# Up projection of the convolutional feed-forward as seven half-size products, gated channels through DRAM, and a down stage that accumulates all channel tiles in eight banks

## The chip, the cores and the metric

The kernel runs on one core of one Trainium2 chip. A core has TensorE (PE, matmuls; PEld is its weight load), VectorE (DVE), ScalarE (ACT), GpSimd (POOL) and SyncE (SP), which here issues the DMAs. SBUF is the working memory, PSUM has eight banks of 128 partitions by 512 float32 into which matmuls accumulate, and DRAM lies outside. The metric is the device time of one execution in microseconds; less is better.

## The reference

One layer of an encoder trunk on 1024 positions with 1024 features: norm, a combined input projection, local and dilated attention, a convolution module and attention to memory tokens, an output projection, and a feed-forward with a convolution. All is float32. The change touches the feed-forward:

```python
f = rms_norm(h, ffn_norm_g[l]) @ w_up[l]          # 1024 x 1024 times 1024 x 5632
f = depthwise_conv(f, ffn_dw_w[l], ffn_dw_b[l])   # 3 taps over positions, one bias a channel
fg, fu = jnp.split(f, 2, axis=-1)                 # 2816 gate channels, 2816 up channels
h = h + (jax.nn.silu(fg) * fu) @ w_down[l]        # 2816 x 1024
```

## The kernel before

Every float32 product is made of three matmuls: each operand is cut into a high part (rounded by ACT to the type `float32r`) and a low part (the operand less its high part, on DVE or POOL), and high x high, high x low and low x high are added in PSUM (`passes`, L140).

Phases 1 and 2 (norm, input projection, attention, convolution, output projection) end with the residual rows in eight SBUF tiles `x_sb` of 128 positions by 1024 features. The last rounds of the output projection add into them from PSUM (`add_out`, L1071). They are not changed.

Phase 3 begins at L1098. Constants are loaded and transposed (L1103 to L1113). For each of the eight tiles of positions, ACT squares and sums the row (L1120), POOL makes the inverse root (L1121 calls `rsqrt`, L163 and L164), DVE scales into a new tile `xn` (L1122), PE transposes it in two halves (L1127), ACT writes the high part of the transpose (L1129) and DVE the low part (L1130). The two tiles `hT` hold this for all positions: [feature, position tile, feature tile, 128 positions].

`up(ct)` (L1137) makes one tile of 128 channels by 1024 positions. Its weights come in two loads of 256 KB (`up_raw`, L1142, two buffers), each cut into a high part by ACT (L1146) and a low part by POOL (L1147). Then 8 feature tiles x 3 parts x 2 halves of the positions make 48 matmuls into two banks (L1152). Three taps of the convolution follow, read from the banks: ACT makes the middle tap with the bias (L1159), DVE the others (L1160 to L1165). There are 44 such tiles of channels: tile ct of the first 22 is a gate, tile 22 + ct what it gates.

`gated(ct)` (L1169) calls `up` for both, ACT applies SiLU (L1171), DVE multiplies (L1173), ACT and DVE cut the product into parts (L1175, L1176), which stay in SBUF.

`down(gs, cts, last)` (L1189) takes two gated tiles at a time: for each position tile and each half of the output features, six matmuls go into one of two banks (L1195), and DVE adds the bank to `x_sb` (L1198): 16 banks for each two tiles, 176 in all. The weights come by L1184 and are cut by L1185 and L1186. The last call sends `x_sb` to the output (L1200). The outer loop (L1202 to L1209) traces `gated` for two tiles and then `down` for the two before.

What sets the order: the program is traced as above, and a scheduler at compile time (`schedule_with_timeline_sim=True`, L1229) puts each engine's instructions in a fixed order. An instruction traced earlier goes first where both are ready by the scheduler's own clock; one that isn't ready lets a later one pass. On the chip each engine then works through its fixed list, and waits at the first instruction whose inputs or buffers aren't there. SP issues the DMAs of phase 3 in one such list, too. Tiles of one tag share a number of buffers (`bufs`), and a new tile waits until the buffer's old readers are done.

Of the kernel before, what the change touches and what calls it, by code (L numbers as in the profile page):

```python
# [9 lines left out]
F = mybir.dt.float32  # L10
# [15 lines left out]
# tiles of 4 KB that the steps share: how many a step may hold, and how many are kept for it  # L26
# [4 lines left out]
# the order of the input projections, the number of them before the first head  # L31
ORDER = "q0 kv g0 g1 v0 q1 v1 q2 m q3".split()
HEAD0 = 2
# steps after each tap of the two tiles of the conv module
PACE = (1, 2)
# tiles of weights whose low parts DVE makes
EARLY = 12
# steps whose instructions go before others, or after them
PRIOS = {"softmax_weights": 1000, "memory_values": -60, "memory_heads": 60, "add_out": 200}
# tiles of mixed rows in the rounds of the output projection  # L40
# [3 lines left out]
def constants():  # L44
    """What depends on shapes alone. Token n = 128 b + 64 e + 16 r + s of a tile stands for
    position 128 b + 64 e + 4 s + r, so that the tokens of one residue mod 4 are runs of 16."""
    c = {}
# [85 lines left out]
def block(tc, a, out):  # L133
# [6 lines left out]
    def passes(n):  # L140
        """(stationary part, moving part) of a float32 product, parts 0: high, 1: low."""
# [19 lines left out]
    def rsqrt(dst, src, scale):  # L161
        """(src * scale + eps) ** -0.5"""
# [61 lines left out]
    def scores(t, ps, mask, nm, den):  # L224
        """one block of 128 queries and 256 keys -> exp(s - max), with -max and the sum"""
# [1007 lines left out]
```

## Time and profile before

| | |
|---|---|
| median of 3 runs | 1340.15 us (1337.95 to 1342.56) |
| span of the profiled execution | 1341.0 us |
| PE, DVE, ACT, POOL busy in it | 94%, 57%, 39%, 38% |
| mean granted TensorE clock | 0.978 |
| first matmul of the up projection, last one of the down projection | 587.5 us, 1335.9 us |
| matmuls of the up projection (L1152), of the down projection (L1195) | 2112, 1056 |

How to read the lines that follow. A page of the profile gives the span, the busy time of each engine and, in 40 slices, the busy tenths and the granted clock (PEclk). A table by stretches (windows) gives for each stretch its length and, for each engine, busy time and (x) instructions begun in it, then the granted clock, the share of the DMA engines and GB/s. A view of one source line gives count, durations in ns as least/median/most, first and last start, and shapes. The timeline gives start in us, duration in us, engine, line, operation, tiles (out<-in), count, and in brackets the idle time before it with what ended it. The list of waits gives total us, times and the longest. A matmul's recorded duration (0.39 us) is longer than the distance to the next one, since they are pipelined: rates are read from counts over stretches.

### The profile page before, as it was taken

The numbers are of one execution on the slowest core, as the hardware profiler recorded it, in microseconds if no ns is written. First come the engines' busy times: TensorE is split into PE (matmuls) and PEld (weight loads), VectorE is DVE, ScalarE is ACT, GpSimd is POOL, SyncE is SP. The second block draws the span as 40 slices with busy tenths as digits, with TensorE's granted clock in tenths as the row PEclk, the third lists the DMA queues.
The fourth block names the chain that finished last, engine by engine and source line by source line (L and its number), as shares of the span: only waits on it lengthen the run. The fifth ranks groups of instructions, "written<-read, shape, count | busy, mean of one in ns | idle before, by whom it ended". The sixth has DMA issues, their size and how long they took to land.

```text
span 1341.0 us, 18723 instructions
## 1 busy us (share of the span) xinstructions
PE 1260.7 (94%) x6895; PEld 1055.1 (79%) x6895; DVE 768.3 (57%) x1530; ACT 521.5 (39%) x1082; POOL 513.2 (38%) x647
## 2 busy tenths in 40 slices
PE   4999897899899989889999999999999999999998
PEld 4988897899768767668888887878787878787876
DVE  7836888786788769883443434434344343434454
ACT  5664163476757656453421313131313131313120
POOL 5723783897655442431410404040405050505010
PEclk9999988999989999999999999999999999999999
DMA  8263426362773331101310303030303030303013
GB/s 271 82 173 95 147 83 197 119 186 80 240 240 95 95 107 36 50 17 33 101 40 0 95 1 94 0 95 0 95 1 94 2 94 0 95 1 87 8 32 126
DMA packets 130039, 114.27 MB, mean 85 GB/s; under 512 B 6850, under 2 KB 110108, under 8 KB 129948
## 3 DMA queue, kind: packets, MB, share of 16 engines
q1 hardware_dynamic: 129948, 113.08, 27.7%
q8 instruction: 54, 0.88, 0.3%
q14 instruction: 37, 0.30, 0.1%
HBM read 87.89 MB, written 25.17 MB: 84 GB/s over the span
## 4 chain that ended last, share of the span: by engine, by line
issue 31%; PE 27%; DMA 17%; POOL 11%; DVE 7%; ACT 5%; SPq 1%; POOLq 0%; ACTq 0%; DVEq 0%
DMA up_raw<-w_up 8%; PE ps_up L1152 7%; PE proj L883 6%; PE proj L1062 5%; POOL up_lo L1147 3%; DMA dn_raw<-w_down 3%; POOL dn_lo L1186 3%; POOL prob L339 2%; PE o L274 2%; PE turn L265 2%; PE s L245 2%; DMA w_raw<-w_in 2%; ACT up_hi L1146 1%; PE ps_dn L1195 1%; DVE conv L946 1%
## 5 line engine op out<-in xcount | busy, mean ns | idle before, releaser
L1152 PE MATMUL ps_up<-hT,up_hi 128*128 128x512 f32 x1408 | 399.8, 396 | 0.0
L1152 PEld LDWEIGHTS ps_up<-hT,up_hi 128*128 128x128 f32 x1408 | 264.2, 188 | 63.6
L1198 DVE TENSOR_TENSOR x<-ps_dn,x 128x512 f32<-128x512 f32 x176 | 120.5, 688 | 204.9 <-PE ps_dn L1195 204.8
L1152 PE MATMUL ps_up<-hT,up_lo 128*128 128x512 f32 x704 | 228.9, 395 | 0.0
L1186 POOL TENSOR_TENSOR dn_lo<-dn_raw,dn_hi 128x512 fp32r<-128x512 f32 x44 | 65.2, 1490 | 406.4 <-ACT dn_hi L1185 406.4
L883 PE MATMUL proj<-w_hi,hnT 128*128 128x256 f32 x896 | 192.0, 302 | 18.3 <-ACT raw L798 6.5
L1147 POOL TENSOR_TENSOR up_lo<-up_raw,up_hi 128x512 fp32r<-128x512 f32 x88 | 121.0, 1377 | 152.6 <-ACT up_hi L1146 148.3
L1160 DVE SCALAR_TENSOR_TENSOR y<-ps_up,fwT,y 128x511 f32<-128x511 f32 x88 | 65.1, 746 | 186.4 <-ACT y L1159 186.4
L883 PEld LDWEIGHTS proj<-w_hi,hnT 128*128 128x128 f32 x896 | 154.0, 204 | 21.1 <-ACT raw L798 7.1
L1152 PEld LDWEIGHTS ps_up<-hT,up_lo 128*128 128x128 f32 x704 | 132.3, 188 | 31.6
L1159 ACT ACTIVATE y<-ps_up,fwT 128x512 f32<-128x512 f32 x88 | 63.8, 771 | 207.3 <-PE ps_up L1152 206.0
L1195 PE MATMUL ps_dn<-dn_hi,g_hi 128*128 128x512 f32 x352 | 138.5, 394 | 4.6 <-DVE x L1198 4.6
L1195 PE MATMUL ps_dn<-dn_lo,g_hi 128*128 128x512 f32 x352 | 138.0, 392 | 0.3 <-POOL dn_lo L1186 0.3
L1195 PE MATMUL ps_dn<-dn_hi,g_lo 128*128 128x512 f32 x352 | 138.1, 392 | 0.0
L883 PE MATMUL proj<-w_lo,hnT 128*128 128x256 f32 x448 | 134.2, 300 | 0.3 <-POOL w_lo L605 0.3
L1062 PE MATMUL proj<-w_hi,mx 128*128 128x512 f32 x256 | 101.0, 431 | 7.5 <-DVE x L1072 5.7
L1146 ACT ACTIVATE up_hi<-up_raw 128x512 fp32r<-128x512 f32 x88 | 55.7, 632 | 125.4 <-DMA up_raw<-w_up 104.5
L339 POOL TENSOR_SCALAR prob<-prob,wc 128x256 f32<-128x256 f32 x128 | 76.6, 620 | 42.6 <-DVE wc L335 42.6
L883 PEld LDWEIGHTS proj<-w_lo,hnT 128*128 128x128 f32 x448 | 91.1, 203 | 1.2 <-POOL w_lo L605 1.0
L617 POOL TENSOR_TENSOR w_lo<-w_raw,w_hi 128x512 fp32r<-128x512 f32 x44 | 64.1, 1469 | 58.7 <-ACT w_hi L615 55.8
L1195 PEld LDWEIGHTS ps_dn<-dn_hi,g_hi 128*128 128x128 f32 x352 | 66.1, 188 | 24.4 <-DVE x L1198 10.0
L946 DVE SCALAR_TENSOR_TENSOR conv<-conv,cwT 128x1009 f32<-128x1009 f32 (+14 forms) x60 | 83.9, 1399 | 0.6
(201 smaller groups left out, 2084.4 us busy)
## 6 DMA issues: line engine op xcount, KB each, us to landing
up_raw<-w_up SPq DMA_DIRECT2D x88, 256.0 KB
dn_raw<-w_down SPq DMA_DIRECT2D x44, 256.0 KB
x<-x SPq DMA_DIRECT2D x16, 512.0 KB
qk_d<-out SPq DMA_DIRECT2D x32, 256.0 KB
qk<-qk_d SPq DMA_DIRECT2D x16, 512.0 KB
w_raw<-w_in SPq DMA_DIRECT2D x40, 128.0 KB
qk<-qk_d SPq DMA_DIRECT2D x16, 256.0 KB
v_d<-out SPq DMA_DIRECT2D x16, 256.0 KB
```

The source lines that it names most:

```text
L339: pool.tensor_scalar(probs[u], probs[u], wc[:, u : u + 1], 0.0, OP.mult, OP.add)
L617: (dve if next(chunk_no) < EARLY else pool).tensor_tensor(lo, raw, f32(hi), OP.subtract)
L883: pe.matmul(ps[:, :256], lhs[i][:, k], c.parts[k][j], start=(k == 0 and i == 0 and j == 0), stop=(k == KT - 1 and i == 1))
L946: dve.scalar_tensor_tensor(acc[:, c0:c1], conv_in[i][:, c0 + k - 15 : c1 + k - 15], w, acc[:, c0:c1], OP.mult, OP.add)
L1062: pe.matmul(ps, mixed[k][i][:, 128 * t : 128 * t + 128], wo[k, half][j], start=(n == 0), stop=(n == 3 * len(ks) - 1))
L1146: act.activation(hi, raw, AF.Copy)
L1147: pool.tensor_tensor(lo, raw, f32(hi), OP.subtract)
L1152: pe.matmul(pss[half], w[k][i], hT[j][:, 4 * half : 4 * half + 4, k], start=(k == 0 and i == 0 and j == 0), stop=(k == KT - 1 and i == 1))
L1160: dve.scalar_tensor_tensor(y[:, c0 + 1 : c1], ps[:, 0:511], tap3[0], y[:, c0 + 1 : c1], OP.mult, OP.add)
L1186: pool.tensor_tensor(w[1][:, cut], raw, f32(w[0][:, cut]), OP.subtract)
L1195: pe.matmul(ps, gs[k][i][:, 128 * t : 128 * t + 128], ws[k][j][:, 512 * half : 512 * half + 512], start=(n == 0), stop=(n == 3 * len(cts) ...
L1198: dve.tensor_tensor(dst, ps, dst, OP.add)
```

## The change

Phases 1 and 2 stay. Phase 3 is written anew; the diff also strips comments, which is left out here.

The up projection of a pair of column tiles (gate tile ct, up tile 22 + ct) is a product of a 2 x 2 matrix of blocks, A (two halves of the positions by two halves of the features), with a 2 x 2 matrix of blocks B (two halves of the features by the two column tiles). It is made in Winograd's form of Strassen's method with seven half-size products in place of eight. Each product is 4 feature tiles x 3 parts = 12 matmuls of 512 positions. The seven left operands (A11, A12, A22 and the sums S1 to S4) are made once for all pairs, after the norm, which now scales `x_sb` in place; the rows before the norm go to DRAM (`h_d`). The seven right operands are B11, B21, B22 and the differences T1 to T4, made by DVE for each pair; all seven are cut into parts, high by ACT, low by POOL. Raw blocks have five buffers of 256 KB, sums and differences four, high and low parts eight each. Banks a, b and c have two buffers, bank d takes one of two single banks in turn. Three banks are accumulated into twice, with a read between (a: p1, then the first half of the gate; c: p5; d: the second half of the up tile). The convolution now reads whole rows from SBUF (`cg`, `cu`) in place of halves in PSUM. The gated tile is not cut but stored to DRAM (`g_d`).

The down stage begins when all 22 pairs are traced. For each half of the positions, all eight banks hold one output block each, over all 22 channel tiles; gated tiles and weights come from DRAM and are cut on the way, the weights in each half anew. A bank is added to the old rows, loaded from `h_d`, once, and the result stored.

```diff
-        hT = [p3r.tile([128, NT, KT, 128], R, name=f"hT{i}") for i in range(2)]
...
+        ops = {nm: [p3r.tile([128, KH, HT], R, name=f"{nm}{i}") for i in range(2)]
+               for nm in ("A11", "A12", "A22", "S1", "S2", "S3", "S4")}
+        ss2 = p3r.tile([128, NT], F, name="ss2")
+        def turn_rows(rows, nm, t):
+            ps = psp.tile([128, KH, 128], F, name="ps_n", tag="turn", bufs=2)
+            for k in range(KH):
+                pe.transpose(ps[:, k], rows[:, 128 * k : 128 * k + 128], ident)
+            hi, lo = (x[:, :, 128 * t : 128 * t + 128] for x in ops[nm])
+            act.activation(hi, ps, AF.Copy)
+            dve.tensor_tensor(lo, ps, f32(hi), OP.subtract)
+        def norm(t):
+            sp.dma_start(h_d[t], x_sb[t])
+            sq = p3r.tile([128, D], F, name="sq2", tag="wide", bufs=2)
+            col = ss2[:, t : t + 1]
+            act.activation(sq, x_sb[t], AF.Square, accum_out=col)
+            rsqrt(col, col, 1.0 / D)
+            xns[t] = x_sb[t]
+            dve.scalar_tensor_tensor(x_sb[t], x_sb[t], col, g_ffn, OP.mult, OP.mult)
         for t in range(NT):
+            norm(t)
+            if t < 4:
+                turn_rows(xns[t][:, 0:512], "A11", t)
+                turn_rows(xns[t][:, 512:1024], "A12", t)
+        for t in range(4):
+            lowr, high = xns[t], xns[t + 4]
+            s1, s2, s3, s4 = (p3r.tile([128, 512], F, name=f"s{i}", tag="wsum", bufs=4) for i in range(4))
+            dve.tensor_tensor(s3, lowr[:, 0:512], high[:, 0:512], OP.subtract)
+            turn_rows(s3, "S3", t)
+            dve.tensor_tensor(s1, high[:, 0:512], high[:, 512:1024], OP.add)
+            turn_rows(s1, "S1", t)
+            dve.tensor_tensor(s2, s1, lowr[:, 0:512], OP.subtract)
+            turn_rows(s2, "S2", t)
+            dve.tensor_tensor(s4, lowr[:, 512:1024], s2, OP.subtract)
+            turn_rows(s4, "S4", t)
+            turn_rows(high[:, 512:1024], "A22", t)
+        xpool.release()
+        pu = tc.alloc_tile_pool(name="pu", bufs=1)
+        BANKS = {"a": ("s", 2), "b": ("proj", 2), "c": ("turn", 2)}
+        def split(src, shape, adder):
+            hi = wpool.tile(shape, R, name="up_hi", tag="w_hi", bufs=8)
+            lo = wpool.tile(shape, R, name="up_lo", tag="w_lo", bufs=8)
+            act.activation(hi, src, AF.Copy)
+            adder.tensor_tensor(lo, src, f32(hi), OP.subtract)
+            return hi, lo
+        def up_weights(ct):
...
+            b11, b12 = load(0, ct), load(0, NF + ct)
+            w["B11"] = split(b11, shape, pool)
+            t1 = comb(b12, b11)
+            b22 = load(1, NF + ct)
+            t3 = comb(b22, b12)
+            t2 = comb(b22, t1)
+            b21 = load(1, ct)
+            w["B21"] = split(b21, shape, pool)
+            w["T3"] = split(t3, shape, pool)
+            w["T1"] = split(t1, shape, pool)
+            t4 = comb(b21, t2)
+            w["T2"] = split(t2, shape, pool)
+            w["B22"] = split(b22, shape, pool)
+            w["T4"] = split(t4, shape, pool)
+        def product(ps, x, w, first, last):
+            for n, (k, i, j) in enumerate(passes(range(KH))):
+                pe.matmul(ps, w[i][:, k], ops[x][j][:, k], start=(first and n == 0), ...)
         def gated(ct):
-            fg = up(ct)
-            act.activation(fg, fg, AF.Silu)
-            fu = up(NF + ct)
+            w = up_weights(ct)
+            cg, cu = (pu.tile([128, S], F, name=nm, tag="c", bufs=3) for nm in ("cg", "cu"))
+            p1, p5, u2, v = (pu.tile([128, 512], F, name=nm, tag="part", bufs=6) for nm in ("p1", "p5", "u2", "v"))
+            pa = bank("a", ct)
+            product(pa, "A11", w["B11"], True, True)
+            act.activation(p1, pa, AF.Copy)
+            pd = bank("d", ct)
+            product(pd, "S3", w["T3"], True, True)
+            product(pa, "A12", w["B21"], False, True)
+            act.activation(cg[:, 0:512], pa, AF.Copy)
+            pc = bank("c", ct)
+            product(pc, "S1", w["T1"], True, True)
+            act.activation(p5, pc, AF.Copy)
+            pb = bank("b", ct)
+            product(pb, "S2", w["T2"], True, True)
+            dve.tensor_tensor(u2, pb, p1, OP.add)
+            pool.tensor_tensor(v, u2, p5, OP.add)
+            dve.tensor_tensor(cu[:, 512:1024], pd, v, OP.add)
+            product(pc, "S4", w["B22"], False, True)
+            dve.tensor_tensor(cu[:, 0:512], pc, u2, OP.add)
+            product(pd, "A22", w["T4"], False, True)
+            dve.tensor_tensor(cg[:, 512:1024], pd, u2, OP.add)
+            ys = []
+            for c, col in ((cu, NF + ct), (cg, ct)):
+                y = p3r.tile(..., tag="wide", bufs=2) if c is cu else pu.tile([128, S], F, name="yg", bufs=2)
+                act.activation(y, c, AF.Identity, scale=tap[1], bias=b)
+                dve.scalar_tensor_tensor(y[:, 1:S], c[:, 0 : S - 1], tap[0], y[:, 1:S], OP.mult, OP.add)
+                dve.scalar_tensor_tensor(y[:, 0 : S - 1], c[:, 1:S], tap[2], y[:, 0 : S - 1], OP.mult, OP.add)
+            act.activation(fg, fg, AF.Silu)
             dve.tensor_tensor(fg, fg, fu, OP.mult)
-            hi, lo = (p3.tile([128, S], R, name=nm, tag=nm, bufs=4) for nm in ("g_hi", "g_lo"))
-            act.activation(hi, fg, AF.Copy)
-            dve.tensor_tensor(lo, fg, f32(hi), OP.subtract)
-            return hi, lo
+            sp.dma_start(g_d[ct], fg)
+        DBANKS = [("s", 2), ("s", 2), ("proj", 2), ("proj", 2), ("turn", 2), ("turn", 2), ("o", 1), ("z", 1)]
+        for part in range(2):
+            banks = [psp.tile([128, 512], F, name="ps_dn", tag=tag, bufs=n) for tag, n in DBANKS]
+            for k in range(NF):
+                gk = split(half_raw(g_d[k][:, HT * part : HT * part + HT]), [128, 512], dve)
+                wk = [split(half_raw(a["w_down"][0, 128 * k : 128 * k + 128, 512 * half : 512 * half + 512]), [128, 512], pool)
+                      for half in range(2)]
+                for n, ps in enumerate(banks):
+                    t, half = n // 2, n % 2
+                    for m, (i, j) in enumerate(((0, 0), (0, 1), (1, 0))):
+                        pe.matmul(ps, gk[i][:, 128 * t : 128 * t + 128], wk[half][j],
+                                  start=(k == 0 and m == 0), stop=(k == NF - 1 and m == 2))
+            for n, ps in enumerate(banks):
+                t, half = 4 * part + n // 2, n % 2
+                r = pu.tile([128, 512], F, name="res", tag="part", bufs=6)
+                sp.dma_start(r, h_d[t][:, 512 * half : 512 * half + 512])
+                dve.tensor_tensor(r, ps, r, OP.add)
+                sp.dma_start(out[128 * t : 128 * t + 128, 512 * half : 512 * half + 512], r)
```

More of the change, by code (lines that the diff above doesn't have):

```diff
@@ L1096, in block @@
     p2.release()
+    h_d = [dpool.tile([128, D], F, name=f"h_d{t}") for t in range(NT)]
+    g_d = [dpool.tile([128, S], F, name=f"g_d{ct}") for ct in range(NF)]
     with (
         tc.tile_pool(name="p3r", bufs=1, side="right") as p3r,
-        tc.tile_pool(name="p3", bufs=1) as p3,
     ):
-        g_ffn = p3r.tile([128, D], F, name="g_ffn", tag="y", bufs=4)
+        g_ffn = p3r.tile([128, D], F, name="g_ffn", tag="wide", bufs=2)
         sp.dma_start(g_ffn, bass.AP(tensor=a["ffn_norm_g"].tensor, offset=0, ap=[[0, 128], [1, D]]))
-        fw = p3r.tile([2 * NF, 4, 128], F, name="fw", tag="y", bufs=4)
+        fw = p3r.tile([2 * NF, 4, 128], F, name="fw", tag="raw", bufs=5)
         sp.dma_start(fw[:, 0:3], a["ffn_dw_w"][0].rearrange("k (t p) -> t k p", p=128))
@@ L1113, in block @@
         dve.tensor_copy(fwT, ps[:, :, : 2 * NF])
[L1115 removed]
+        HT = S // 2
+        KH = KT // 2
+        ops = {nm: [p3r.tile([128, KH, HT], R, name=f"{nm}{i}") for i in range(2)]
+               for nm in ("A11", "A12", "A22", "S1", "S2", "S3", "S4")}
         ss2 = p3r.tile([128, NT], F, name="ss2")
[L1117 to L1130 removed]
@@ new lines, in product, with bank @@
+        def product(ps, x, w, first, last):
+            for n, (k, i, j) in enumerate(passes(range(KH))):
+                pe.matmul(ps, w[i][:, k], ops[x][j][:, k], start=(first and n == 0), stop=(last and n == 3 * KH - 1),
+                          skip_group_check=not first)
+        def bank(which, ct):
+            if which == "d":
+                return psp.tile([128, 512], F, name="ps_d", tag="oz"[ct % 2], bufs=1)
+            tag, n = BANKS[which]
+            return psp.tile([128, 512], F, name="ps_" + which, tag=tag, bufs=n)
@@ L1171, in gated @@
             act.activation(fg, fg, AF.Silu)
-            fu = up(NF + ct)
             dve.tensor_tensor(fg, fg, fu, OP.mult)
-            hi, lo = (p3.tile([128, S], R, name=nm, tag=nm, bufs=4) for nm in ("g_hi", "g_lo"))
-            act.activation(hi, fg, AF.Copy)
-            dve.tensor_tensor(lo, fg, f32(hi), OP.subtract)
-            return hi, lo
-        def down_weights(ct):
-            w = [p3.tile([128, D], R, name=nm, tag=nm, bufs=3) for nm in ("dn_hi", "dn_lo")]
-            for half in range(2):
-                cut = slice(512 * half, 512 * half + 512)
-                raw = wpool.tile([128, 512], F, name="dn_raw", tag="w_raw", bufs=2)
-                sp.dma_start(raw, a["w_down"][0, 128 * ct : 128 * ct + 128, cut])
-                act.activation(w[0][:, cut], raw, AF.Copy)
-                pool.tensor_tensor(w[1][:, cut], raw, f32(w[0][:, cut]), OP.subtract)
-            return w
@@ L1189, in down @@
-        def down(gs, cts, last):
-            ws = [down_weights(ct) for ct in cts]
-            for t in range(NT):
-                for half in range(2):
-                    ps = psp.tile([128, 512], F, name="ps_dn", tag="proj", bufs=2)
-                    for n, (k, i, j) in enumerate(passes(range(len(cts)))):
-                        pe.matmul(ps, gs[k][i][:, 128 * t : 128 * t + 128], ws[k][j][:, 512 * half : 512 * half + 512],
-                                  start=(n == 0), stop=(n == 3 * len(cts) - 1))
-                    dst = x_sb[t][:, 512 * half : 512 * half + 512]
-                    dve.tensor_tensor(dst, ps, dst, OP.add)
-                if last:
-                    sp.dma_start(out[128 * t : 128 * t + 128, :], x_sb[t])
@@ L1202, in block, with half_raw @@
-        before = None
-        for c in range(NF // 2):
-            cts = [2 * c, 2 * c + 1]
-            gs = [gated(ct) for ct in cts]
-            if before:
-                down(*before, False)
-            before = (gs, cts)
-        down(*before, True)
-    xpool.release()
+            sp.dma_start(g_d[ct], fg)
+        for ct in range(NF):
+            gated(ct)
+        DBANKS = [("s", 2), ("s", 2), ("proj", 2), ("proj", 2), ("turn", 2), ("turn", 2), ("o", 1), ("z", 1)]
+        def half_raw(src):
+            t = p3r.tile([128, 512], F, name="dn_raw", tag="raw", bufs=5)
+            sp.dma_start(t, src)
+            return t
@@ L1211, in block @@
+        pu.release()
     wpool.release()
```

62 lines of the change are left out of this document (16 added, 46 removed).

## The prediction

> **What bounds the kernel now.** I read the page first, then the table by stretches around phase 3, then the counts of its two matmul lines, PE's waits, and last the views of single lines.
>
> ```profile
> span 1341.0 us, 18723 instructions
> PE 1260.7 (94%) x6895; PEld 1055.1 (79%) x6895; DVE 768.3 (57%) x1530; ACT 521.5 (39%) x1082; POOL 513.2 (38%) x647
> ```
> ```profile
> 560.00:570.00 10.00, 5.88 (x16) 3.81 (x15) 8.24 (x9) 3.96 (x6) 3.22 (x2) 0.70 0.37 114
> 570.00:587.00 17.00, 13.64 (x67) 9.34 (x66) 16.32 (x24) 9.61 (x19) 6.57 (x12) 0.98 0.01 1
> ...
> 735.00:1290.00 555.00, 550.35 (x2360) 442.21 (x2359) 226.34 (x360) 140.95 (x199) 143.53 (x100) 1.00 0.16 48
> 1290.00:1336.00 46.00, 45.74 (x198) 36.33 (x196) 26.16 (x39) 3.66 (x5) 2.54 (x2) 1.00 0.19 76
> ```
> ```profile
> 734.40:748.40 14.00, 13.98 (x60) 11.27 (x60) 1.00 0.26 76
> ```
> ```profile
> 1292.00:1312.00 20.00, 20.00 (x88) 15.83 (x87) 1.00 0.00 0
> 1314.00:1334.00 20.00, 19.74 (x86) 15.64 (x85) 1.00 0.40 158
> ```
> ```profile
> PE ps_dn L1195 <- DVE x L1198: 4.6, 7, 1.6
> ```
>
> From 735 to 1290 us PE is busy 550.35 of 555 us at full clock, while DVE is busy 41%, ACT and POOL 26%. The third fence is L1152 alone, in a stretch without down matmuls: 14.00 / 60 = 0.2333 us each. The fourth is L1195 alone: 20.00 / 88 = 0.2273 us. PE's longest wait in phase 3 comes to 4.6 us. So phase 3 is bound by the number of matmuls, and only what shortens or interrupts that stream counts.
>
> **Matmuls removed.** A pair of column tiles takes 96 matmuls now and 7 x 12 = 84 then; over 22 pairs 2112 become 1848. 264 x 0.2333 = **-61.6 us**. The down projection keeps its 1056.
>
> **Their rate.** L1152 streams four runs of 128 positions, L1195 one run of 512; the new products stream one run of 512. If that is the 0.0060 us between the rates, 1848 x 0.0060 = 11.1 us more go; if not, nothing. I take **-5**.
>
> **Down stage.** Each bank is added once, 16 adds for 176: the 4.6 us of waiting end, since each new bank is left alone for the other seven (7 x 3 x 0.2273 = 4.8 us) before it is needed. What is new is the feed: 24 matmuls (5.45 us) use three raw blocks of 256 KB, 144 GB/s, where 158 GB/s took 0.40 of the DMA engines.
>
> ```profile
> 760.15 2.77 DMA dn_raw<-w_down
> ```
> ```profile
> L1184 SPq DMA_DIRECT2D dn_raw<-w_down x44: 327/328/346, 641.1 to 1287.4; - x44
> ```
> ```profile
> L1146 ACT ACTIVATE up_hi<-up_raw x88: 618/632/650, 491.7 to 1232.1; 128x512 fp32r<-128x512 f32 x88
> ```
> ```profile
> L1147 POOL TENSOR_TENSOR up_lo<-up_raw,up_hi x88: 1274/1293/2249, 492.4 to 1232.8; 128x512 fp32r<-128x512 f32 x88
> ```
>
> A raw buffer turns in 0.33 + 2.77 + 0.63 + 1.29 = 5.0 us (6.0 with POOL's slowest), so five supply three blocks in 3.0 to 3.6 us, under 5.45. The feed binds only from a turn of 9.1 us. I take **-4**, ends -5 and +8.
>
> **Head of the stage.** All sums of rows must stand before the S products.
>
> ```profile
> 589.69 0.48 PE L1152 MATMUL ps_up<-hT,up_hi 128*128 128x512 f32 x1
> ...
> 600.92 0.60 PE L1127 MATMUL ps_n<-small,xn 128*128 128x128 f32 x4
> 601.28 0.48 PE L1152 MATMUL ps_up<-hT,up_hi 128*128 128x512 f32 x1
> ```
> ```profile
> 586.75 0.68 DVE L1072 TENSOR_TENSOR x<-proj,x 128x512 f32<-128x512 f32 x1
> 587.34 1.28 DVE L1122 SCALAR_TENSOR_TENSOR xn<-x,ss,g_ffn 128x1024 f32<-128x1024 f32 x1
> 588.54 0.68 DVE L1130 TENSOR_TENSOR hT<-ps_n,hT 128x512 fp32r<-128x512 f32 x1
> 589.14 0.68 DVE L1072 TENSOR_TENSOR x<-proj,x 128x512 f32<-128x512 f32 x1
> ...
> 592.93 0.68 DVE L1130 TENSOR_TENSOR hT<-ps_n,hT 128x512 fp32r<-128x512 f32 x1
> ```
>
> DVE is already full here (16.32 of 17 us), with starts 0.60 us apart, 1.20 for the norm. Up to about 593 us it does what it did. Then one norm, 20 low parts and 16 sums are left, 1.2 + 36 x 0.60 = 22.8 us, so the last operand stands near 616 us, 619 at the operations' own lengths, more with weight differences between. The last position tile takes nine of these steps, so its S3 is ready some 4 us before that, at 612 to 615. Until then PE has only A11 of two pairs (bank a has two buffers): p1, which A12 waits for, lies in the old rows' space, last read near the end too. Before, PE streamed from 589.7 with eight groups of transposes (0.36 us each by the rows) between. I let the stream begin at 615.5, for the weight differences; that loses 25.8 - 24 x 0.2333 - 8 x 0.36 = 17.3; with the store to `h_d`, which the in-place norm must await, I take **+18**. Ends: +10 if some sums are made before 593, +35, twice the estimate, if the space of the old rows or of the new operands comes free late. The first raw blocks may stand behind the eight stores on SP, but B11 is wanted only with A11, near 589.
>
> **The exposed chain in each pair.** A22 accumulates onto bank d, which must first be read: S2's end, u2 (DVE), v (POOL), the second half of cu (DVE), then PE.
>
> ```profile
> L1198 DVE TENSOR_TENSOR x<-ps_dn,x x176: 675/691/694, 683.8 to 1336.4; 128x512 f32<-128x512 f32 x176
> ```
> ```profile
> L1122 DVE SCALAR_TENSOR_TENSOR xn<-x,ss,g_ffn x8: 1275/1276/2073, 572.4 to 598.1; 128x1024 f32<-128x1024 f32 x8
> ```
> ```profile
> L617 DVE TENSOR_TENSOR w_lo<-w_raw,w_hi x12: 676/688/1218, 21.6 to 77.9; 128x512 fp32r<-128x512 f32 x12
> ```
> ```profile
> L1159 ACT ACTIVATE y<-ps_up,fwT x88: 760/771/779, 599.5 to 1291.8; 128x512 f32<-128x512 f32 x88
> ```
> ```profile
> L1171 ACT ACTIVATE y<-y x22: 1042/1059/1065, 628.8 to 1285.9; 128x1024 f32<-128x1024 f32 x22
> ```
> ```profile
> 756.35 1.30 POOL L1147 TENSOR_TENSOR up_lo<-up_raw,up_hi 128x512 fp32r<-128x512 f32 x1 [2.09 <-ACT up_hi L1146]
> 757.88 2.25 POOL L1147 TENSOR_TENSOR up_lo<-up_raw,up_hi 128x512 fp32r<-128x512 f32 x1 [0.22 <-ACT up_hi L1146]
> ```
> ```profile
> 756.36 0.69 DVE L1198 TENSOR_TENSOR x<-ps_dn,x 128x512 f32<-128x512 f32 x1
> 756.96 0.74 DVE L1165 SCALAR_TENSOR_TENSOR y<-ps_up,fwT,y 128x512 f32<-128x512 f32 x1
> 757.74 1.23 DVE L1173 TENSOR_TENSOR y<-y 128x1024 f32<-128x1024 f32 x1
> ```
>
> Alone the chain is 0.69 + 1.29 + 0.69 = 2.7 us and a few hops; S4 covers 12 x 0.2333 = 2.8. But engines may be taken: DVE by a tap (1.28), POOL by a low part (1.29). So it lasts 2.8 to 5.4, and shows 0 to 2.5 us a pair, where PE's list holds no matmul of the next pair in that place. The list does mix work so:
>
> ```profile
> 734.19 0.39 PE L1195 MATMUL ps_dn<-dn_hi,g_lo 128*128 128x512 f32 x1
> 734.42 0.63 PE L1152 MATMUL ps_up<-hT,up_lo 128*128 128x512 f32 x2
> ```
>
> I take 0.8 us, nearer the low end because A11 of the next pair is there to be put in: 22 x 0.8 = **+18**, ends 0 and 55.
>
> The other engines are loaded per pair (PE 84 x 0.2333 = 19.6 us): DVE 4 x 0.69 weight differences + 4 x 0.69 from banks + 4 x 1.28 taps (as long as the norm's L1122, of the same operation) + 1.23 gate = 11.8; POOL 8 x 1.29 = 10.3; ACT 7 x 0.63 + 3 x 0.77 + 3 x 1.06 = 9.9. So these are hidden, as are the reads of banks a (S3 between p1 and A12: 2.8 us) and c (S2 between p5 and S4). Behind v in POOL's list stand low parts of the next pair, with eight buffers for seven operands some five products (14 us) ahead. On SP the store of the gated tile waits for the gate, and the next raw blocks stand behind it with the same lead. Should that cover go, each late block costs its 2.77 us. The traffic, 1.0 MB in and 0.5 MB out in 19.6 us, is 80 GB/s, half of the 158 shown.
>
> The last two fences show the catch: POOL takes 1.30 us beside DVE operations that read PSUM, but 2.25 beside the product of two SBUF tiles. Such operations grow from 1.23 x 2 a pair (this product and g_lo, of the same shape) to 2.75 + 5.1 + 1.23 = 9.1 us; with POOL's 10.3 that is 19.4 of PE's 19.6. The Trainium skill ("SBUF — State Buffer", section "SBUF: two separate sides") has a rule against this change: GpSimd and a VectorE operation with two SBUF inputs share a port pair under an exclusive lock, and the later one blocks. The trace agrees: the 2.25 us are 1.29 and nearly all of the 1.09 us overlapped.
>
> **Seams and tail.** From up to down and between the two halves: **+2** (0 to 6), since all but the last gated tiles lie in DRAM by then.
>
> ```profile
> 1336.35 0.69 DVE L1198 TENSOR_TENSOR x<-ps_dn,x 128x512 f32<-128x512 f32 x1 [0.67 <-PE ps_dn L1195]
> ```
>
> After 1337.04 the last 512 KB took to 1341.0; 256 KB take **-1** (to 0).
>
> **Sum.** -61.6 - 5 - 4 + 18 + 18 + 2 - 1 = -33.6 on 1341.0: 1307.4. The median lies 0.85 below this execution, so 1306.6, said as 1307.
>
> **Rivals.**
> - *The port pair binds* (chance 0.14). For: 19.4 of 19.6 us leaves nothing for an in-order list that idles. Against: weights are made some 14 us ahead, so both lists can shift without PE noticing. With a tenth idle a pair takes 21.4, 1.8 more: 22 x 1.8 = 40 in place of 18 gives 1329.
> - *A22 waits out the chain* (0.12), the slower end. Without the exposed term the sum is -51.6, so it decides from 51.6 / 22 = 2.35 us a pair. If v stands behind a low part stretched to 2.25 us and is stretched itself, and u2 behind a tap: 1.28 + 0.69 + 2.25 + 2.25 + 0.69 - 2.8 = 4.4 at worst; at 3.4 it is 1341 - 52 + 75 = 1364. For: the fixed list cannot know these stretches. Against: PE's waits are now 4.6 us in all under the same scheduler.
> - *Nothing shows* (0.10): contiguous rate, +10 head, 0.2 us a pair: -61.6 - 11.1 - 5 + 10 + 4.4 + 0 - 1 = -64.3, 1277.
> - *The clock falls* (0.03). In 560 to 570 us PE, busy 5.88 of 10, got 0.70:
>
> ```profile
> 563.84 0.71 PE L1062 MATMUL proj<-w_hi,mx 128*128 128x512 f32 x1 [1.19 <-DVE mx L280]
> 566.51 0.80 PE L1062 MATMUL proj<-w_hi,mx 128*128 128x512 f32 x1 [1.96 <-DVE x L1072]
> ```
>
> If breaks hold the up stage (431 us) at 0.9, it costs 48: 1341 - 52 + 18 + 48 = 1355. The Trainium skill ("TensorE: Matmul & The Clock Gate", Part 1) halves the clock after an idle window of about 3.4 us; by that, breaks of one or two microseconds would cost nothing, though the two rows are such breaks in the stretch at 0.70.
> - *The feed binds the down stage* (0.03): a turn of 10 us makes 6.0 of 5.45, 44 x 0.55 = +24, 1331.
>
> **How the numbers follow.** The forecast has 0.58, most of it 1285 to 1330. A measurement here tells 0.3%, 4 us. Faster: 0.56 of it, 0.11 of the port's, 0.10 where nothing shows and 0.03 where the feed binds, 0.80. Within 1336 to 1344: 0.02 of it, 0.03 of the port's, 0.01 of the chain's just past its point, 0.06. Slower: the chain's 0.11 and the clock's 0.03, 0.14. The range, 1279 to 1344, leaves out these 0.14 and half of "nothing shows".
>
> **What would show it.** Right: up matmuls near 0.228 to 0.233 us over full stretches; the stream full from about 615 us; 20 to 21 us a pair; a down stage near 240 us with PE full; POOL lengths bimodal. Wrong: a break over 2.35 us before each A22; POOL or DVE busy over 90% in the up stage; PE waiting for low parts; clock under 1 after 620 us.

## The result, and the profile after

| | before | after |
|---|---|---|
| median of 4 runs | 1340.53 us | 1318.91 us (1316.23 to 1320.34) |
| ratio, 95% interval | | 0.9841 (0.9822 to 0.986) |
| profiled execution, span | 1341.0 us | 1316.23 us, span 1314.5 us |

Faster by 21.6 us; the forecast was 1307, the range 1279 to 1344. The page of after:

```profile
span 1314.5 us, 19197 instructions
PE 1205.7 (92%) x6679; PEld 1007.3 (77%) x6679; DVE 905.2 (69%) x1420; ACT 608.6 (46%) x1248; POOL 760.1 (58%) x779
```

PE lost 55 us of busy time, but 2% of its share too: part of what the removed matmuls gave is idle time now. The table by stretches shows where:

```profile
570.00:587.00 17.00, 5.71 (x23) 3.55 (x21) 12.43 (x12) 11.72 (x22) 11.54 (x17) 0.62 0.51 175
587.00:597.00 10.00, 6.22 (x23) 4.76 (x24) 8.82 (x13) 3.18 (x6) 1.86 (x2) 0.50 0.00 1
...
700.00:1050.00 350.00, 338.56 (x1432) 267.43 (x1431) 277.96 (x221) 149.85 (x222) 234.41 (x138) 1.00 0.26 78
1080.00:1180.00 100.00, 100.00 (x442) 82.79 (x442) 23.89 (x19) 30.34 (x54) 56.61 (x39) 1.00 0.48 155
```

From 570 to 587 us DVE, full in that stretch before, is busy 12.43 of 17, and the granted clock is 0.62, then 0.50. In the up stage (700 to 1050) PE misses 11.4 us of 350. The down stage (last row) has no gap: 442 matmuls in 100.00 us, by their starts one every 0.2267 us.

The four longest in PE's list of waits from 570 us on:

```profile
PE ps_d L1206 <- DVE cu L1233: 11.4, 17, 0.7
PE ps_n L1129 <- DVE A L1132: 9.4, 8, 3.1
PE ps_n L1129 <- DVE S L1132: 8.1, 13, 1.1
PE ps_n L1115 <- DMA fw<-ffn_dw_w: 5.2, 1, 5.2
```

The first is the exposed chain, in 17 of the 22 pairs (from 700 us on); the others are the head.

The two executions had drifted apart by 6.0 us when attention ended (last matmul of L274 at 556.7 and 550.7), before anything that was changed. So the stages are counted from there, by the first and last starts in the views of the matmul lines; "down alone" and the last two columns are experiments, below:

| us after the last matmul of attention | before | after | down alone | two pools | three edits |
|---|---|---|---|---|---|
| last matmul of the output projection | 31.8 | 19.5 | 31.1 | 28.0 | 28.3 |
| last up matmul | 734.2 | 520.9 | 527.6 | 510.6 | 497.0 |
| last down matmul | 779.2 | 755.1 | 767.0 | 744.5 | 730.7 |
| end | 784.3 | 763.8 | 771.1 | 752.6 | 734.9 |

784.3 - 763.8 = 20.5 us, about the 21.6 of the medians. This gain is made up of five terms:

- count of matmuls: -61.6;
- down stage, and breaks of the old alternation of up and down: -11.2 (what the other terms leave; measured alone below);
- head: +32.1 (the stream is full 74.1 us after attention for 33.0; 9.0 us are taken off for 26 matmuls and eight groups of transposes that lie before it; two matmuls lay before it in the old kernel too, which is 0.5 us);
- breaks in the pairs: +16.6;
- tail: +3.6.

### The profile page after: what moved, and what is told of

Read it like the earlier page. It is cut to its first block, busy times and chain, and to the rows that moved or that the text cites. A ratio compares the mean times of both kernels' runs of the same rounds, so it can differ in the third digit from the quotient of the medians.

```text
span 1314.5 us, 19197 instructions
## 1 busy us (share of the span) xinstructions
PE 1205.7 (92%) x6679; PEld 1007.3 (77%) x6679; DVE 905.2 (69%) x1420; ACT 608.6 (46%) x1248; POOL 760.1 (58%) x779
## 4 chain that ended last, share of the span: by engine, by line
PE 55%; DVE 13%; POOL 9%; issue 8%; DMA 7%; ACT 7%; SPq 1%; POOLq 0%; DVEq 0%; ACTq 0%
PE ps_dn L1271 17%; PE proj L1062 6%; PE ps_c L1206 6%; PE ps_d L1206 6%; PE ps_a L1206 5%; PE proj L883 4%; PE ps_b L1206 3%; DMA w_raw<-w_in 2%; PE o L274 2%; DVE up_sum L1183 2%; POOL r L164 2%; PE turn L265 2%; PE proj L909 2%; DVE yg L1248 2%; PE s L245 2%
## 5 line engine op out<-in xcount | busy, mean ns | idle before, releaser
L1171 POOL TENSOR_TENSOR up_lo<-up_sum,up_hi 128x512 fp32r<-128x512 f32 x88 | 164.3, 1877 | 62.0 <-ACT up_hi L1170 58.4
L1171 POOL TENSOR_TENSOR up_lo<-dn_raw,up_hi 128x512 fp32r<-128x512 f32 x88 | 131.2, 1510 | 115.3 <-ACT up_hi L1170 102.1
L1170 ACT ACTIVATE up_hi<-dn_raw 128x512 fp32r<-128x512 f32 x132 | 75.3, 622 | 162.8 <-issue 119.6
L1271 PE MATMUL ps_dn<-up_lo,up_hi 128*128 128x512 f32 x352 | 136.9, 389 | 0.1
L1271 PE MATMUL ps_dn<-up_hi,up_lo 128*128 128x512 f32 x352 | 136.5, 389 | 0.0
L1271 PE MATMUL ps_dn<-up_hi 128*128 128x512 f32 x352 | 133.4, 389 | 0.0
L1206 PE MATMUL ps_a<-A,up_hi 128*128 128x512 f32 x352 | 115.2, 399 | 0.0
L1206 PE MATMUL ps_c<-S,up_hi 128*128 128x512 f32 x352 | 110.9, 396 | 0.7 <-DVE S L1132 0.7
L1206 PEld LDWEIGHTS ps_a<-A,up_hi 128*128 128x128 f32 x352 | 66.7, 190 | 16.1
L1271 PEld LDWEIGHTS ps_dn<-up_lo,up_hi 128*128 128x128 f32 x352 | 66.1, 188 | 14.3 <-POOL up_lo L1171 0.6
```

Of the source, the lines that this page charges most:

```text
L1170: act.activation(hi, src, AF.Copy)
L1171: adder.tensor_tensor(lo, src, f32(hi), OP.subtract)
L1206: pe.matmul(ps, w[i][:, k], ops[x][j][:, k], start=(first and n == 0), stop=(last and n == 3 * KH - 1), skip_group_check=not first)
L1271: pe.matmul(ps, gk[i][:, 128 * t : 128 * t + 128], wk[half][j], start=(k == 0 and m == 0), stop=(k == NF - 1 and m == 2))
```

## The experiments

Ratios are to the kernel before on the same chip; "after" means 0.9841.

**The tail.** After's last two adds wait for their old rows. The last matmul, the last load, and the last add:

```profile
1305.79 0.39 PE L1271 MATMUL ps_dn<-up_hi,up_lo 128*128 128x512 f32 x1
1306.48 0.61 SPq L1276 DMA_DIRECT2D res<-h_d  x1
1310.83 0.69 DVE L1277 TENSOR_TENSOR res<-ps_dn,res 128x512 f32<-128x512 f32 x1 [2.51 <-DMA res<-h_d]
```

A row of `res` can be loaded only when one of six buffers has been stored. Experiment: the last two in another tag.

```diff
-r = pu.tile([128, 512], F, name="res", tag="part", bufs=6)
+r = pu.tile([128, 512], F, name="res", tag="part" if n < 6 else "c", bufs=6 if n < 6 else 3)
```

> The last two of the eight old-row blocks are loaded into buffers of another tag (the freed convolution rows), in place of waiting for the first two results to be stored. If the tail is held by these buffers (in the changed kernel 8.3 us from PE's last matmul to the end, against 4.7 before): the last additions follow PE at once, the tail falls to about 4.5 us, 1315.3 us against 1318.9. If the landing of the last stores sets the end whatever the loads do: at most 1 us less, 1318 to 1319.

Measured: 0.9809 (0.9794 to 0.9824), 0.0032 of 1340 or 4.3 us below after. The timeline's end:

```profile
1298.59 5.45 DVE L1277 TENSOR_TENSOR res<-ps_dn,res 128x512 f32<-128x512 f32 x8 [9.65 <-PE ps_dn L1271]
```

All eight adds run together, and the end comes 4.7 us after the last matmul for 8.7. The buffers were the cause.

**The breaks in the pairs.** One pair in the timeline of after, DVE, POOL and the matmul that waits:

```profile
875.01 1.28 DVE L1243 SCALAR_TENSOR_TENSOR yg<-cg,fwT,yg 128x1023 f32<-128x1023 f32 x1
875.58 4.12 POOL L1171 TENSOR_TENSOR up_lo<-up_sum,up_hi 128x512 fp32r<-128x512 f32 x2 [1.38 <-ACT up_hi L1170]
876.33 2.20 DVE L1244 SCALAR_TENSOR_TENSOR yg<-cg,fwT,yg 128x1023 f32<-128x1023 f32 x1
878.45 1.79 DVE L1183 TENSOR_TENSOR up_sum<-up_raw 128x512 f32<-128x512 f32 x1
880.16 0.68 DVE L1183 TENSOR_TENSOR up_sum<-up_raw,up_sum 128x512 f32<-128x512 f32 x1
880.28 1.72 POOL L1171 TENSOR_TENSOR up_lo<-up_raw,up_hi 128x512 fp32r<-128x512 f32 x1 [0.59 <-ACT up_hi L1170]
880.76 2.31 DVE L1248 TENSOR_TENSOR yg<-yg,yu 128x1024 f32<-128x1024 f32 x1
883.00 0.68 DVE L1231 TENSOR_TENSOR u<-ps_b,p 128x512 f32<-128x512 f32 x1
883.82 1.30 POOL L1232 TENSOR_TENSOR v<-u,p 128x512 f32<-128x512 f32 x1 [1.82 <-DVE u L1231]
885.16 0.69 DVE L1233 TENSOR_TENSOR cu<-ps_d,v 128x512 f32<-128x512 f32 x1 [1.48 <-POOL v L1232]
885.90 0.73 PE L1206 MATMUL ps_d<-A,up_hi 128*128 128x512 f32 x2 [0.66 <-DVE cu L1233]
```

S2's last matmul ends at 876.6. The chain itself (883.00 to 885.9) takes 2.9 us, as the forecast had it; but u2 starts 6.4 us late, behind a tap, two differences and the gate product. Those that ran beside POOL's low parts took 2.20, 1.79 and 2.31 us; without POOL they take 1.28, 0.69 and 1.23. PE had 37 matmuls (8.6 us) of other products to put between, not quite enough. Two readings: DVE's list is simply too long there, or the port pair stretches it. Two experiments take POOL's low parts away: onto DVE, which makes DVE's list longer, or onto ACT, as a copy in the low part's place (this leaves out the subtraction of the high part).

```diff
-            adder.tensor_tensor(lo, src, f32(hi), OP.subtract)
+            (dve if shape[1] == KH else adder).tensor_tensor(lo, src, f32(hi), OP.subtract)
```

> All seven low parts of a pair's weights are made by DVE, none by POOL; POOL keeps v. Port theory (u2 comes late because DVE's taps, differences and gate product ahead of it are stretched while POOL reads SBUF): DVE has 16.6 us of 19.6 a pair but no stretch, taps 1.28 and not 2.2 us, the break ahead of A22 falls from 0.94 to about 0.3 us a pair, 10 to 15 us less, 1304 to 1309. List theory (u2 is late because of what stands ahead of it in DVE's list, stretched or not): more stands ahead of it now, the break grows by one or two low parts, 0.7 to 1.4 us a pair, 15 to 30 us more, 1334 to 1349.

```diff
-            adder.tensor_tensor(lo, src, f32(hi), OP.subtract)
+            if shape[1] == KH:
+                act.activation(lo, src, AF.Copy)
+            else:
+                adder.tensor_tensor(lo, src, f32(hi), OP.subtract)
```

> The low parts of the up weights are made by ACT as a copy (the subtraction of the high part is left out), so POOL has only v. Port theory: DVE's operations with two SBUF inputs return to 1.28 and 0.69 us, the break ahead of A22 nearly goes, 15 to 20 us less, 1299 to 1304. List theory: the same operations stand ahead of u2, 1316 to 1322. ACT has 14.3 us of 19.6 a pair.

Measured: 0.9733 (0.9718 to 0.9748) and 0.9723 (0.9706 to 0.9739), 14.5 and 15.8 us below after. The table by stretches of the one on DVE:

```profile
700.00:1050.00 350.00, 350.00 (x1502) 281.78 (x1501) 276.99 (x346) 165.37 (x232) 33.00 (x22) 1.00 0.26 82
```

DVE makes 346 operations in place of 221 in the same busy time (276.99 for 277.96), and PE has no break. Groups by line from 640 to 1040 us, after first, then with the low parts on DVE, show why:

```profile
L1183 DVE TENSOR_TENSOR up_sum<-up_raw 128x512 f32<-128x512 f32 x38 | 48.2, 1267 | 10.6 <-POOL up_lo L1171 10.6
L1244 DVE SCALAR_TENSOR_TENSOR yg<-cg,fwT,yg 128x1023 f32<-128x1023 f32 x19 | 41.8, 2200 | 0.7
L1171 POOL TENSOR_TENSOR up_lo<-up_sum,up_hi 128x512 fp32r<-128x512 f32 x78 | 148.9, 1918 | 32.0 <-ACT up_hi L1170 28.4 <-PE ps_a L1206 3.6
```
```profile
L1183 DVE TENSOR_TENSOR up_sum<-up_raw 128x512 f32<-128x512 f32 x38 | 26.2, 689 | 0.7
L1244 DVE SCALAR_TENSOR_TENSOR yg<-cg,fwT,yg 128x1023 f32<-128x1023 f32 x20 | 25.6, 1279 | 0.0
L1171 DVE TENSOR_TENSOR up_lo<-up_raw,up_hi 128x512 fp32r<-128x512 f32 x60 | 41.0, 684 | 0.0
```

A low part costs 0.68 us on DVE and on average up to 1.92 on POOL, and from POOL it also took 0.6 to 0.9 us from the DVE operation beside it. That DVE's list is simply too long is refuted: it is longer now, and the breaks are gone. What is shown is that these operations of DVE and POOL lengthen each other; that they share a port, the trace does not show by itself. The Trainium skill ("SBUF — State Buffer", section "SBUF: two separate sides") has this as an exclusive lock whose loser waits; the trace agrees, and shows that both sides lose in turn: the tap grows from 1.28 to 2.20, the low part from 1.29 to a mean of 1.92.

**The head.** In after the gain row is asked for right behind the last matmul of the output projection, and DVE idles until the loads that start there have landed (the trace names the last of them, the taps `fw`):

```profile
570.24 0.39 PE L1062 MATMUL proj<-w_hi,mx 128*128 128x512 f32 x1
570.71 1.06 ACT L1140 ACTIVATE sq<-x 128x1024 f32<-128x1024 f32 x1 [14.72 <-PE proj L1062]
570.77 0.33 SPq L1107 DMA_DIRECT2D g_ffn<-ffn_norm_g  x1
575.81 1.29 DVE L1143 SCALAR_TENSOR_TENSOR x<-x,ss,g_ffn 128x1024 f32<-128x1024 f32 x1 [4.46 <-DMA fw<-ffn_dw_w]
```

Before, norms began beside the last round (572.4, of 588.5). The new pool takes 139 KB a partition for 81. By the addresses that the compiler gave, the old one lay over the attention stage's memory alone; the new one reaches down over the output projection's operands (`mx`) as well. First theory: each tile waits only for what lay in its own place; then it helps to place operands needed late over `mx`, and the gain row over the attention stage's memory. The edit moves the allocation of `ops` ahead of `g_ffn`, last-needed first:

```diff
+        ops = {nm: [...] for nm in ("S4", "S3", "S2", "S1", "A22", "A12", "A11")}
         g_ffn = p3r.tile([128, D], F, name="g_ffn", tag="wide", bufs=2)
...
-        ops = {nm: [...] for nm in ("A11", "A12", "A22", "S1", "S2", "S3", "S4")}
```

> Only the order of allocation is changed: the fourteen operand tiles, S4 first, come ahead of the gain row, the squares and the raw blocks, so that late tiles and not early ones lie where the output projection's last rows were. Space theory (gain row and squares wait for the last matmul of the output projection because they lie on its rows; DVE then idles from 571.3 to 575.8): norms begin 5 us earlier and run beside the last round, the up stream is full 5 to 10 us earlier, 1309 to 1314. Work theory (DVE has too many steps in the head, whenever it starts): under 2 us, 1317 to 1319.

Measured: 0.9866 (0.9847 to 0.9885), no gain; the gain row is asked for at 570.2, the last matmul of the round is at 569.7. The wait of its load, in after and then in this run:

```profile
SPq L1107 <- PE proj L1062: 0.7, 1, 0.7
```
```profile
SPq L1111 <- PE proj L1062: 0.7, 1, 0.7
```

In this run the gain row lies where only tiles of the attention stage had been, and its load still waits for a matmul of the output projection. The first theory falls. Second: the whole pool waits for everything that it lies over. The edit cuts it in two, and the first part, with the gain row, no longer lies over `mx`:

```diff
+        early = ("A11", "A12", "S3")
-               for nm in ("A11", "A12", "A22", "S1", "S2", "S3", "S4")}
+        ops = {nm: [...] for nm in early}
...
+        p3s = tc.alloc_tile_pool(name="p3s", bufs=1, side="right")
+        ops.update({nm: [...] for nm in ("S1", "S2", "S4", "A22")})
         for t in range(4):
             lowr, high = xns[t], xns[t + 4]
```

> Change after with the memory of the stage cut in two: gain row, taps, A11, A12 and S3 in a first pool about as large as the old one (74 KB a partition), S1, S2, S4 and A22 in a second that is allocated only behind the norms. Theory of the pool: the 139 KB pool overlaps that of the attention stage and so the gain row waits for the last matmul of the output projection; cut in two, the gain row comes at about 566 us as before the change, the squares and norms start beside the last round of the output projection, and the stream is full 4 to 8 us earlier: ratio to before 0.978 to 0.981 (after: 0.984). Rival: the head is bound by DVE's work of 36 steps after the last sums of the residual, so the norms start earlier but the stream is full within 2 us of after's: ratio 0.983 to 0.985.

Measured: 0.976 (0.9738 to 0.9782), 10.9 us below after, more than expected. Its first norm and its stretch from 570 us:

```profile
564.40 1.28 DVE L1143 SCALAR_TENSOR_TENSOR x<-x,ss,g_ffn 128x1024 f32<-128x1024 f32 x1
```
```profile
570.00:587.00 17.00, 12.11 (x58) 9.32 (x59) 17.00 (x24) 8.12 (x15) 8.42 (x10) 0.90 0.36 145
```

The first norm starts 13.3 us after attention's end for 25.1, DVE is full, and the up stage ends 10.3 us earlier (510.6 for 520.9). The place of a pool set a third of the head's cost.

The clock is a second matter. In after it is 0.50 from 575 us to about 597, behind PE's break of 5.21 us (the wait for the taps). With two pools it falls later, behind a break of 2.59 us:

```profile
590.40 0.63 PE L1129 MATMUL ps_n<-small,s 128*128 128x128 f32 x4 [2.59 <-DVE S L1132]
```
```profile
590.00:595.00 5.00, 3.70 (x16) 0.67 0.00 0
595.00:600.00 5.00, 4.16 (x17) 0.50 0.00 0
```

It stays at 0.50 to 610 us, with PE busy four fifths of the time. The Trainium skill ("TensorE: Matmul & The Clock Gate", Part 1) halves the clock after an idle window of some 3.4 us: after's 5.21 us agrees, and so do the breaks of 0.7 us in the pairs, which left it at 1.00; the 2.59 us do not, and there the measurement decides. In the run with all three edits (below) it fell at about 603 us, where no break since 596 us had been longer than 0.63 us and PE had been busy 1.58 of the last 3.3 us. What the falls cost the head, no run here shows.

What is left of the head might lie in its order: position tile by position tile, all operands are ready late. The next edit traces the sums operand by operand, S3 of all four tiles first; it also writes S2 and S4 over rows that are no longer needed, in place of buffers of their own.

> Change after with the sums traced operand by operand (S3 of all four position tiles, then S1, S2, S4, A22) in place of position tile by position tile. Theory: S3's and S1's products of the first pairs can then run while DVE still makes S2 and S4, so that some 24 to 36 of the first matmuls (5.6 to 8.4 us) lie beside the sums: ratio to before 0.978 to 0.980. Rival: p1, which the products behind A11 need for their banks to come free, lies in memory that is free only after the last use of the old rows, and PE's list is the scheduler's, so little moves: 0.983 to 0.985.

Measured: 0.9829 (0.9799 to 0.986), no difference that can be told from after. The pool is whole in this run, so its late start could hide a gain; the edit comes again below with the pool in two.

**The down stage alone.** The kernel before, with the gated tile sent to DRAM and the new down stage behind the old up projection:

```diff
-            hi, lo = (p3.tile([128, S], R, name=nm, tag=nm, bufs=4) for nm in ("g_hi", "g_lo"))
...
+            sp.dma_start(g_d[ct], fg)
...
+        for part in range(2):
+            banks = [psp.tile([128, 512], F, name="ps_dn", tag=tag, bufs=n) for tag, n in DBANKS]
...
+                r = x_sb[t][:, 512 * half : 512 * half + 512]
+                dve.tensor_tensor(r, ps, r, OP.add)
```

> The old up projection with the gated tile stored to DRAM, and the new down stage behind it (rows kept in SBUF, so no h_d); the Strassen part is left away. The forecast's term for the down stage was -4 us (-5 to +8), its seam +2, its tail -1: ratio to before about 0.998. The accounting of the two traces says instead that the down matmuls gain 1.9 us by their rate (1056 x 0.0018) and 9.3 us by breaks of PE that the old alternation of up and down had: about -11 us, ratio 0.992. If DRAM traffic or the lost cover of DVE and ACT work between the stages costs something, the ratio is 1.00 or above. In all cases the up matmuls stay at 0.2333 us.

Measured: 0.9899 (0.9879 to 0.9918), 13.5 us: by itself more than half of the whole gain. PE in the up and the down stretch of it:

```profile
600.00:1000.00 400.00, 400.00 (x1722) 1.00 0.24 75
1100.00:1200.00 100.00, 100.00 (x443) 1.00 0.43 144
```

Neither has a gap, and the down stage feeds itself. So, by subtraction, the seven products, 61.6 us of matmuls less, brought only the other 8 us: head, breaks and tail ate the rest.

**The rate.** The up products stayed at 0.2333 us with their operand contiguous. Six series of 96 matmuls, appended to after, take the operands from different places (one execution, of which only the rates are read):

```diff
+        for g in range(8):
+            pb7 = psp.tile([128, 512], F, name="r1", tag=DBANKS[g % 6][0], bufs=2)
+            for m in range(12):
+                pe.matmul(pb7, gk[m % 3 // 2][:, ...], ops["S1"][m % 3 % 2][:, m // 3 % 4], start=(m == 0), stop=(m == 11))
...
```

> Change after, followed by six series of 96 matmuls each whose results are not used, on an otherwise idle core: r1 stationary from the weights' memory, moving from an operand of the up products, 12 to a bank (as the up products); r2 the same with moving from the weights' memory; r3 as r2 with 3 to a bank (as the down stage); r4 as r1 with 3 to a bank; r5 stationary and moving both from operands of the up products, 12 to a bank; r6 stationary from those, moving from the weights' memory. If the place of the moving operand makes the up products 0.2333 and the down products 0.2267 us, r1, r4, r5 take 0.2333 and r2, r3, r6 0.2267. If the number of matmuls to a bank does, r1, r2, r5, r6 take 0.2333 and r3, r4 0.2267. If it is what other engines do at the time, all six take 0.2267 or less. Time: 6 x 96 x 0.23 = 132 us more than after.

Stretches inside r1, r2, r3, r4, r5 and r6, PE alone:

```profile
1310.50:1332.50 22.00, 22.00 (x96) 1.00 0.25 84
1333.00:1354.00 21.00, 21.00 (x94) 1.00 0.00 1
1355.00:1374.50 19.50, 19.50 (x88) 1.00 0.00 1
1379.00:1395.50 16.50, 16.50 (x73) 1.00 0.00 1
1406.00:1415.00 9.00, 9.00 (x41) 1.00 0.00 0
1421.00:1442.00 21.00, 21.00 (x92) 1.00 0.00 1
```

A stretch also counts a matmul at its edge, so the rate is taken from the first to the last start inside: r1 0.2333, r2 0.2268, r3 0.2267, r4 0.2334, r5 0.2272 (over 40 matmuls), r6 0.2333. None of the three expectations is met. Fast, then, where both operands come from one pool (r2, r3, r5), slow where they don't. The number to a bank and the other engines, idle here, do not matter. Whether the pool does, the runs e13 and e15 below try.

**The three edits that helped, together.**

> Change after with the three edits that helped by themselves: the last two blocks of old rows in buffers of their own (-3.5 us), the up weights' low parts on DVE (-13.5), the memory of the stage in two pools (-10.9). If the three lie in different stretches (end, pairs, head), they add up: -27.9 us from after, ratio to before 0.984 - 0.021 = 0.963. If DVE, which takes over 0.69 x 7 us a pair, is then what the head waits for, the head's gain is partly lost: 0.966 to 0.970.

Measured: 0.9614 (0.9592 to 0.9636), 1289.40 us: they add up, 30.4 us for the 29.7 of the three measured alone. With the sums operand by operand besides:

> As e12_three, with the sums traced operand by operand. Alone that edit gave 0.9829 for 0.9841, no difference. If it was hidden behind the late release of the pool, S3's and S1's products now run beside the later sums: 3 to 6 us below e12_three, 0.959 to 0.961. If DVE's steps bind the head whatever their order, the same as e12_three within 2 us.

Measured: 0.961 (0.9578 to 0.9643), 1289.50 us, the same. DVE is full in it, 44.9 of the 45 us from 570 to 615 us, so in this order its steps bind the head. In the other order it is busy 41.3 of them and waits for transposes in between; that DVE alone binds there is not shown.

**Operands in one pool.** The parts of the up weights move to the first of the two pools of left operands, where A11, A12 and S3 lie; the other four lie in the second.

```diff
-            hi = wpool.tile(shape, R, name="up_hi", tag="w_hi", bufs=8)
+            where, tag, n = (p3r, "p", 4) if shape[1] == KH else (wpool, "w", 8)
+            hi = where.tile(shape, R, name="up_hi", tag=tag + "_hi", bufs=n)
...
-                t = p3r.tile([128, KH, 128], F, name="up_raw", tag="raw", bufs=5)
+                t = wpool.tile([128, KH, 128], F, name="up_raw", tag="w_hi", bufs=8)
```

> As e12_three, but the parts of the up weights (4 buffers each for high and low, for 8) lie in the pool of the left operands, and raw blocks and differences in the weights' old memory; the down stage keeps its parts in the weights' old memory, with 4 buffers for raw blocks. Theory of the place, from the six series: matmuls whose two operands lie in the same pool take 0.2267, in different ones 0.2333; then the 1848 up matmuls take 0.2267 and the time falls by 1848 x 0.0066 = 12.2 us below e12_three: ratio about 0.954. Rival: the series differed for another reason (the data, the order of reading), the up matmuls stay at 0.2333 and the ratio is that of e12_three or above it. In both cases four buffers for seven operands may cost some breaks, which the trace would show as PE waiting for the parts of the weights.

Measured: 0.9635 (0.9609 to 0.9661), no gain, and the same count of matmuls in a stretch as with the three edits. By their starts, A11, A12 and S3, now in one pool with the weights, take 0.2331 to 0.2333 us like the rest. The theory of the pool falls. What else the series had in common are the addresses that the compiler gave: weights' parts start at 1248 modulo 2048 bytes, left operands of the up products at 1984, so that those of a slow series differ by 32 modulo 64. In this run they still did (2016 against 1280 or 1984). The kernel before fits too: its up products read 1248 and 1856, which differ by 32 modulo 64, and take 0.2333; both operands of its down stage start at 1248.

**Operands moved by 32 bytes.**

```diff
         ss2 = p3r.tile([128, NT], F, name="ss2")
+        pad = p3r.tile([128, 8], F, name="pad")
```

> As e12_three, plus one unused tile of 32 bytes a partition behind the first operands, which moves all left operands of the up products by 32 bytes and nothing else of them. Theory of the alignment: in the series r1 and r4 the two operands of a matmul started at addresses that differ by 32 modulo 64 bytes (parts of weights at 32, left operands at 0), in r6 too (0 and 32), and they took 0.2333; in r2, r3 (both 32) and r5 (both 0) they agreed, and took 0.2267. In e13_same_side they still differed (weights at 32, operands at 0), which is why it stayed at 0.2333; the down stage's agree. Now all agree: the 1848 up matmuls take 0.2267, and the time falls by 1848 x 0.0066 = 12.2 us below e12_three's, ratio 0.952. Rival: the series had another reason; nothing changes, 0.2333 and 0.961.

Measured: 0.9572 (0.9543 to 0.9602), 1281.81 us. PE from 700 to 900 us, in the three edits, with one pool, and moved by 32 bytes:

```profile
700.00:900.00 200.00, 200.00 (x859) 1.00 0.26 80
```
```profile
700.00:900.00 200.00, 200.00 (x859) 1.00 0.27 81
```
```profile
700.00:900.00 200.00, 200.00 (x870) 1.00 0.27 83
```

11 more matmuls in 200 us, where 25 would be all at 0.2267. By the ratios this run is 5.6 us below the three edits, with intervals that overlap. The timeline of the last has both rates, S2 (`ps_b`) and then A11 or A12 (`ps_a`), a row each three matmuls apart:

```profile
814.37 0.62 PE L1210 MATMUL ps_b<-S,up_hi 128*128 128x512 f32 x2
...
815.05 0.63 PE L1210 MATMUL ps_a<-A,up_hi 128*128 128x512 f32 x2
...
815.75 0.63 PE L1210 MATMUL ps_a<-A,up_hi 128*128 128x512 f32 x2
```

Three of S2 take 0.68 us, three of A 0.70: 0.2267 and 0.2333. Moved by 32 bytes, S1, S2, S4 and A22, which lie in the second pool, start at 1248 modulo 2048, as the weights do. A11, A12 and S3, in the first, start at 1952, 704 = 5 x 128 + 64 away. By all starts from 640 to 1020 us, A11, A12 and S3 take 0.2333 us a matmul, S2 takes 0.2266, and S1, S4 and A22 take 0.2285 on average: each of these three follows a slow product, and only after some five spacings (from one start to the next) of 0.226 to 0.236 does it settle at 0.2267. So agreement modulo 64 isn't enough, and agreement of the tiles' starts modulo 2048 is. Within a tile the slices start at multiples of 512 bytes, which doesn't matter.

The gain follows: 22 x 12 x (0.0067 + 3 x 0.0048) = 5.6 us, as much as the ratios say. The up stage ends 7.5 us earlier after attention (489.5 for 497.0), but 2.3 of these (ten matmuls) are there already 110 us after attention, before the full stretches. Whether 128, 256 or 512 is the modulus, and whether moving the first pool by 64 more brings the other 5 us, wasn't tried; nor what in the chip makes it so.

## Why the prediction was right, and where not

The time lies in the range, 12 us above the forecast, and the likeliest case, faster with part of the gain lost, is what happened. By its steps, counted from attention's end:

- *Matmuls removed*, -61.6: right. 84 of 0.2333 a pair; the loss is elsewhere.
- *Their rate*, -5: failed. It stayed at 0.2333 with one run of 512. The step took the four runs of the moving operand for what slows L1152; what the runs show in its place is where both operands start.
- *Down stage, seam, tail*, -4, +2, -1: mis-sized. Alone the new down stage gives -13.2 between the traces (784.3 to 771.1). The step counted only PE's listed waits of 4.6 us. From the first up to the last down matmul it is 736.9 for 748.4 us: 11.5. By the starts in the two traces, 6.1 of these are breaks at the 82 changes from an up to a down matmul, and 4.7 lie among the down matmuls: 974 spacings of 0.2315 us on average, where the new stage has 0.2267. Each short group began with some five longer spacings, as behind a slow product above. The new tail, in the whole change, is +3.6, for the buffers of `res`. The feed didn't bind.
- *Head*, +18: mis-sized, 32.1. "Up to about 593 us it does what it did" failed: the pool made every norm wait for the output projection, some 10 us (e8). The rest, 22, is near the 18, though the clock of 0.50 is in it and was not in the step. The end of +35 named the cause, "if the space of the old rows or of the new operands comes free late".
- *Exposed chain*, +18: 16.6, the size right and the reason half, so in part by luck. The chain is 2.9 us and PE's list does put other products into its place; that this didn't suffice came from the rival's mechanism, the port pair, at a smaller dose: DVE was busy 79% and POOL 67% from 700 to 1050 us, so nothing was full, but u2 stood behind stretched operations. Weights made ahead do not help where the result of the pair itself stands in that list.

The errors add up to 13: head +14, rate +5, tail +4.6, against the down stage's -7 and the seam's and chain's -3.

Of its signs, a pair takes 20.5 us and the down stage is full, as said; the stream is full 15 us later than said. Of the rivals, A22's wait is there in 17 pairs, at 0.9 us far below its point of 2.35; the clock fell in the head alone, and not in the up stage; the feed and "nothing shows" did not come.

## What to carry to other kernels

Removing work from the bound engine pays only where the new schedule keeps it fed: here 61.6 us of matmuls became 8, and three small edits outside the product (low parts off POOL, a pool cut in two, two more buffers) gave 30 more (0.9841 to 0.9614). Ask of each new operation which operations of other engines it will run beside and lengthen, and of a new, larger pool what it lies over. Do one part of a change alone: the part that seemed minor, the down stage, was most of the gain.

## What the runs showed of the hardware that wasn't expected

Back-to-back matmuls of 128x512 of `float32r` take 0.2267 us where the tiles of the stationary and the moving operand start at the same address modulo 2048 bytes. They take 0.2333 in every run here where these starts differ by 32 modulo 64, and in the one case where they differ by 704 (64 modulo 128). The pool doesn't decide it. An unused tile of 32 bytes gave the best kernel of the study, 1281.81 us, 0.9572 (0.9543 to 0.9602) of the kernel before. And a DVE operation with two SBUF inputs beside a POOL operation loses time as POOL does: 1.28 became 2.20 us, where POOL's 1.29 became 1.92 on average.
